# Eight byte distances between weight buffers and slots, and wider value matmuls in latent attention

## The chip, the cores and the metric

The kernel runs on one core of one Trainium2 chip. The metric is the device time of one execution in microseconds, as the median of several runs. Engines: PE (TensorE) multiplies matrices, with its weight loads shown apart as PEld; ScalarE (ACT) and VectorE (DVE) work element by element; SyncE (SP) issues the transfers.

## What is computed

One token sequence of 512 positions and 1024 features goes through two blocks in 32-bit floats. The first has two layers: a gated feed-forward, a mixer (sliding-window attention, a recurrent unit, a short convolution) and a second feed-forward. The second has one layer: a mixer of latent attention (over the 512 positions and 256 of a context) and gated linear attention, and a feed-forward with a convolution. Cut to what the change touches:

```python
def swiglu(h, w_gu, w_down):
    gu = h @ w_gu
    g, u = jnp.split(gu, 2, axis=-1)
    return (jax.nn.silu(g) * u) @ w_down
...
    def one_block(qs):
        qn, qr = qs
        s = jnp.einsum('bqhd,bkhd->bhqk', qn, k_nope) + jnp.einsum('bqhr,bkr->bhqk', qr, k_rope)
        p = jax.nn.softmax(s.astype(jnp.float32) * MLA_SCALE, axis=-1).astype(v.dtype)
        return jnp.einsum('bhqk,bkhd->bqhd', p, v)
```

Latent attention has 8 heads with values of 64 features, 512 queries in four tiles of 128, and 768 keys in six tiles of 128.

## The kernel before

**Matmuls in three parts.** Every operand of a large matmul is held as a high part (rounded to `float32r`, a copy by ScalarE, L506) and a low part (the rest, a subtraction by VectorE, L507). A product of two is three matmuls, in `mm`: low weights with high activations (L499), high with low (L500), high with high (L501), each with 128 rows, 128 output columns and up to 512 moving columns. The weights are the stationary operand, the activations the moving one.

**Weights.** They come from memory in chunks of 128 x 1024 (eight slices of 128 columns) into the four `raw` buffers, are split into one of four `whi` and one of four `wlo` buffers (pools `hip` and `lop`, `split_next`, L456 on), and are used by 24 matmuls: eight slices, three each. A chunk is split as soon as an older one is retired.

**Slots.** Activations lie in 36 tiles `r0` to `r35` of 128 x 512 (2048 bytes in each partition), which are taken and given back in a queue, in pairs of high and low part. Eight extra slots are slices of one tile `xr` in a pool `xp` that is opened last; at other times that pool holds plain floats (`xf`).

**Places in a partition.** Pools follow one another in the order in which they are opened: `cp` (the arena of 61,440 bytes, the 36 slots, and then 5,376 bytes of small tiles), `rawp`, `hip`, `lop`, `sm` (12 small tiles, 384 bytes), and `xp` behind. Tiles are rounded up to 32 bytes.

**Latent attention** (`Mixer2.mla`). For the values, `tokmajor` makes six tiles of 128 keys x 512 (L1430 to L1432 and the copy behind them). A unit is a head and a tile of 128 queries; 32 units run in the order of head pair, query tile, head. In a loop over `n`, unit `n` gets its scores (L1745, L1746: six matmuls into a pair of PSUM banks), its maximum (L1749, L1750, VectorE) and its exponentials with their sum (L1752, shown as L400, ScalarE); unit `n - 1` is divided by its sum (L1756, L1757, VectorE); unit `n - 2` is turned, by six transposes on PE (L1762) and one copy by ScalarE (L1765) into a buffer of its own. Every second step `values` (L1773) multiplies two turned units with the values of their two heads, 12 matmuls of 128 columns with 64 output columns each, which write the two halves of the partitions of one bank; the trace has two records for each. Behind the fourth query tile the bank is split into a pair of slots. In between come the keys and queries of the next head pair (`prep_k`, `prep_q`, `split_k`). `Mixer1.values` (L1167) has matmuls of the same kind with 512 columns.

Of the kernel before, what the change touches and what calls it, by code (L numbers as in the profile page):

```python
# [9 lines left out]
F32 = mybir.dt.float32  # L10
F32R = mybir.dt.float32r
AF = mybir.ActivationFunctionType
# [15 lines left out]
P = 128  # L28
S = 512
# [172 lines left out]
class Arena:  # L202


    def __init__(self):
        self.tiles = []
        self.free = []
        self.cur = 0
# [133 lines left out]
class Prog:  # L342
# [4 lines left out]
    def __init__(self, es, tc, d, out):  # L347
        self.es, self.tc, self.d, self.out = es, tc, d, out
        nc = self.nc = tc.nc
        self.T, self.V, self.A = nc.tensor, nc.vector, nc.scalar  # L350

        def mk(n, b, **k):
            return es.enter_context(tc.tile_pool(name=n, bufs=b, **k))

        cp = self.cp = mk("cp", 1)
        self.rawp = mk("rawp", self.RAW)
        self.hip = mk("hip", self.WB)
        self.lop = mk("lop", self.WB)
        self.sm = mk("sm", 12)
        self.banks = Banks(tc)  # L360
        self.park = mk("dp", 1, space=bass.MemoryType.DRAM).tile([KD, P, S], F32, name="park")
        self.logits = mk("dl", 1, space=bass.MemoryType.DRAM).tile([16, P, S], F32, name="logits")
        self.F = Arena()
        self.F.add(cp.tile([P, self.NF * 512], F32, name="farena"), self.NF * 2)
        self.R = Slots([cp.tile([P, S], F32R, name=f"r{i}")[:, :] for i in range(36)])
        self.RX = Slots()
        self.xpool = None
        self.vecs = cp.tile([P, d["vecs"].shape[1]], F32, name="vecs")
        self.cst = cp.tile([P, 3 * P], F32, name="cst")
        self.ident = self.cst[:, 0:P]  # L370
        self.maskf, self.maskb = self.cst[:, P:2 * P], self.cst[:, 2 * P:3 * P]
        self.ones = cp.tile([P, P], F32, name="ones")
        self.eps = cp.tile([P, 1], F32, name="eps")
        self.sinks = cp.tile([P, 16], F32, name="sinks")
        self.nsink = cp.tile([P, 16], F32, name="nsink")
        self.mod = [cp.tile([P, 72], F32, name=f"mod{l}") for l in range(2)]
        self.mod2 = cp.tile([P, 48], F32, name="mod2")
        self.modc = cp.tile([P, 16], F32, name="modc")
        self.crow = [None] * 3
        self.units = []  # L380
        self.ready = {}
        self.ld = self.sp = self.tk = self.rt = self.nsplit = 0
        self.bg = []
        self.users, self.loader = [], None
# [69 lines left out]
    def split_next(self):  # L454
        u = self.units[self.sp]
        if self.ld <= self.sp:  # L456
            self.load_next()
        kind, ap, key, raw = u
        n = ap.shape[-1]
        if kind == "w":  # L460
            h = self.hip.tile([P, 1024], F32R, name="whi", tag="whi")
            lo = self.lop.tile([P, 1024], F32R, name="wlo", tag="wlo")
            self.split(raw[:, :n], h[:, :n], lo[:, :n])
            self.ready[self.nsplit] = (key, h, lo)
            self.nsplit += 1
        else:
            self.mod_unit(key, raw)
            if self.sp < EARLY:
                raw.done()
        u[3] = None  # L470
        self.sp += 1
        ahead = self.RAW + (4 if self.sp < EARLY - 8 else 0)
        while self.ld < len(self.units) and self.ld < self.sp + ahead:
            self.load_next()
# [707 lines left out]
class Mixer2:  # L1182
# [236 lines left out]
    def tokmajor(self, keys, nk, toks, one=False):  # L1419

        p = self.p
        out = []

        def part(acc, w, j, xs):
            hi, lo = w
            for kk in range(nk):
                xh, xl = xs[j * nk + kk]
                s = slice(kk * 512, (kk + 1) * 512)
                a, z = j + kk == 0, j == len(keys) - 1 and kk == nk - 1
                p.T.matmul(acc[:, :], lhsT=xl, rhs=hi[:, s], start=a, stop=False)  # L1430
                p.T.matmul(acc[:, :], lhsT=xh, rhs=lo[:, s], start=False, stop=False)
                p.T.matmul(acc[:, :], lhsT=xh, rhs=hi[:, s], start=False, stop=z)  # L1432

        def copy(t, acc):
            o = p.f(512, one)
            if t % 2:
                p.V.tensor_copy(o[:, :], acc[:, :])
            else:
                p.A.activation(o[:, :], acc[:, :], AF.Copy)
            acc.done()  # L1440
            out.append(o)

        if one:
            w = p.take("x", *keys[0])
            for t, xs in enumerate(toks):
                acc = p.banks.get()
                part(acc, w, 0, xs)
                copy(t, acc)
                p.bgstep()
            p.retire()  # L1450
            return out
        accs = [p.banks.get() for _ in toks]
        for j, k in enumerate(keys):
            w = p.take("x", *k)
            for t, xs in enumerate(toks):
                part(accs[t], w, j, xs)
            p.retire()
        for t, acc in enumerate(accs):
            copy(t, acc)
        return out  # L1460
# [212 lines left out]
    def mla(self):  # L1673
        p = self.p
        V, A, T = p.V, p.A, p.T
        p.bg.append(self.g_qn())
        p.bgstep()
        toks = [[(a[:, t * P:(t + 1) * P], b[:, t * P:(t + 1) * P]) for a, b in self.kvn] for t in range(4)]
# [32 lines left out]
        ks = p.rslots(6)  # L1711
# [8 lines left out]
        def split_k(i, j):  # L1720
            r = slice(64 * j, 64 * j + 64)
            p.split(kb[i][r, :768], kh[j][r], kl[j][r])
            if j:
                kb.pop(i).done()
# [30 lines left out]
        def divide(s, m):  # L1755
            V.reciprocal(m[:, 2:3], m[:, 1:2])  # L1756
            V.tensor_scalar(s[:, :768], s[:, :768], m[:, 2:3], None, op0=MUL)  # L1757

        def turn(s):
            b = p.banks.pair()  # L1760
            for k in range(6):
                T.transpose(b[:, k * P:(k + 1) * P], s[:, k * P:(k + 1) * P], p.ident)  # L1762
            s.done()
            t = p.f(768)
            A.activation(t[:, :768], b[:, :768], AF.Copy)  # L1765
            b.done()
            return t

        def values(i, qt, p0, p1, o):
            for k in range(6):  # L1770
                for j, pt in enumerate((p0, p1)):
                    hd = 2 * i + j
                    T.matmul(o[64 * j:64 * j + 64, qt * P:(qt + 1) * P], lhsT=self.vt[k][:, hd * 64:hd * 64 + 64],  # L1773
                             rhs=pt[:, k * P:(k + 1) * P], start=k == 0, stop=k == 5)
            p0.done()
            p1.done()

        units = [(i, qt, j) for i in range(4) for qt in range(4) for j in range(2)]
        st, pt, o = {}, {}, {}
        prep_q(0)  # L1780
        p.banks.mode(2)
        split_k(0, 0)
        split_k(0, 1)
        for n in range(len(units) + 4):
            if n < len(units):
                i, qt, j = units[n]
                st[n] = scores(i, qt, j)
                if qt == 3 and i < 3:
                    split_k(i + 1, j)
                if (qt, j) == (3, 1):  # L1790
                    for jj in range(2):
                        for b in qs.pop((i, jj)):
                            b.done()
            if 1 <= n <= len(units):
                divide(*st[n - 1])
            if 2 <= n < len(units) + 2:
                pt[n - 2] = turn(st.pop(n - 2)[0])
            m = n - 3
            if 1 <= m <= len(units) and m % 2 == 1:
                i, qt, _ = units[m]  # L1800
                if qt == 0:
                    o[i] = p.banks.get()
                values(i, qt, pt.pop(m - 1), pt.pop(m), o[i])
                if qt == 3:
                    pr, = p.rpairs(1)
                    self.om.append(pr)
                    ob = o.pop(i)
                    p.split(ob[:, :], pr[0][:, :], pr[1][:, :])
                    ob.done()
            if n < len(units):  # L1810
                i, qt, j = units[n]
                if (qt, j) == (1, 1) and i < 3:
                    prep_k(i + 1)
                if (qt, j) == (2, 0) and i < 3:
                    prep_q(i + 1)
        p.banks.mode(8)
        for b in ks + self.vt + [self.tb]:
            b.done()
        p.drop(self.qn)
        p.drop(self.kvs)  # L1820
# [230 lines left out]
```

## Time and profile before

| | |
|---|---|
| median of 3 runs | 2720.52 us (2720.5 to 2720.85) |
| the profiled execution | 2719.37 us, of which its span is 2717.6 us |
| PE busy | 2686.7 us, 99% of the span, 13874 matmuls |
| VectorE, ScalarE busy | 1671.1 us (61%), 1022.1 us (38%) |
| mean granted TensorE clock | 0.995 |

Busy times of PE are unions over matmuls that overlap in the pipeline, so the duration of one matmul is longer than the step from its start to the start of the next one. A row of the timeline has the start in us from the start of the span, the duration, the engine, the line and the operation, and what it writes and reads.

### The profile page before, as it was taken

The page shows a single profiled execution, that of the slowest core. Times are in us where ns is not written, and L with a number is a line of the kernel's source. Part 1 is how long each engine was busy: PE and PEld are TensorE (multiplying, and loading weights), DVE is VectorE, ACT ScalarE, POOL GpSimd, SP SyncE. Part 2 cuts the span into 40 slices and gives each one's busy share as a digit, 9 for nine tenths or more (in the row PEclk, how much of TensorE's full clock was granted, in tenths as well). Part 3 has the DMA queues.
Part 4 walks back from the last instruction along what each step waited for, and adds up shares of the span by engine and source line. Part 5 has one row for each costly group of instructions (what it writes and reads, how often), then busy time and mean ns, then how long its engine had stood idle before and what let it go on. Part 6 is the DMA issues. An engine that isn't in the chain of part 4 may idle for free.

```text
span 2717.6 us, 34690 instructions
## 1 busy us (share of the span) xinstructions
PE 2686.7 (99%) x13874; PEld 2262.7 (83%) x13874; DVE 1671.1 (61%) x2854; ACT 1022.1 (38%) x1603; POOL 0.2 (0%) x4
## 2 busy tenths in 40 slices
PE   9999999999999999999999999999999999999998
PEld 7888897898888988888879888888888788988887
DVE  8554468664444744446866865474576675785666
ACT  3322237442222422223654232253444564432322
POOL 0000000000000000000000000000000000000000
PEclk9999999999999999999999999999999999999999
DMA  7544444344444444444423665423222203233231
GB/s 286 194 140 149 152 140 137 109 147 143 147 149 145 138 160 142 147 145 153 144 74 112 204 216 190 144 92 117 76 95 67 93 32 120 86 102 100 88 101 61
DMA packets 105890, 355.85 MB, mean 131 GB/s; under 512 B 11776, under 2 KB 14976, under 8 KB 105472
## 3 DMA queue, kind: packets, MB, share of 16 engines
q1 hardware_dynamic: 105728, 353.64, 39.4%
q8 instruction: 108, 1.77, 0.3%
q14 instruction: 54, 0.44, 0.1%
HBM read 345.21 MB, written 8.39 MB: 130 GB/s over the span
## 4 chain that ended last, share of the span: by engine, by line
PE 93%; DVE 4%; ACT 2%; issue 1%; DMA 0%; SPq 0%; DVEq 0%; ACTq 0%
PE pb L499 28%; PE pb L501 28%; PE pb L500 28%; PE pb L1773 1%; PE pd L1745 1%; PE pd L1762 1%; ACT farena L400 1%; PE pb L617 1%; PE pb L1167 1%; PE pb L1640 0%; DVE wlo L507 0%; PE pb L1114 0%; PE pb L1151 0%; PE pb L581 0%; PE pb L1430 0%
## 5 line engine op out<-in xcount | busy, mean ns | idle before, releaser
L499 PE MATMUL pb<-r,wlo 128*128 128x512 f32 (+1 forms) x3360 | 1236.6, 369 | 1.2 <-DVE wlo L507 1.1
L500 PE MATMUL pb<-r,whi 128*128 128x512 f32 (+1 forms) x3360 | 1229.2, 367 | 0.0
L501 PE MATMUL pb<-r,whi 128*128 128x512 f32 (+1 forms) x3360 | 1228.8, 366 | 0.0
L506 ACT ACTIVATE whi<-raw 128x1024 fp32r<-128x1024 f32 (+2 forms) x450 | 464.2, 1032 | 828.1 <-issue 448.5
L499 PEld LDWEIGHTS pb<-r,wlo 128*128 128x128 f32 x3360 | 632.8, 189 | 114.4 <-issue 7.6
L500 PEld LDWEIGHTS pb<-r,whi 128*128 128x128 f32 x3360 | 633.6, 189 | 103.7 <-issue 1.9
L501 PEld LDWEIGHTS pb<-r,whi 128*128 128x128 f32 x3360 | 633.4, 189 | 103.8 <-issue 0.2
L507 DVE TENSOR_TENSOR wlo<-raw,whi 128x1024 fp32r<-128x1024 f32 (+2 forms) x450 | 535.7, 1191 | 211.8 <-ACT whi L506 210.4
L511 DVE CUSTOM_DVE_ANT_0 raw<-raw,farena 128x1024 f32<-128x1024 f32 x176 | 215.2, 1223 | 194.9 <-DMA raw<-wmod 139.7
L676 DVE SCALAR_TENSOR_TENSOR farena<-pb,mod,farena 128x512 f32<-128x512 f32 (+1 forms) x176 | 114.9, 653 | 210.5 <-PE pb L501 210.2
L499 PE MATMUL pb<-xr,wlo 128*128 128x512 f32 (+1 forms) x520 | 188.1, 362 | 0.0
L501 PE MATMUL pb<-xr,whi 128*128 128x512 f32 (+1 forms) x520 | 187.4, 360 | 0.0
L500 PE MATMUL pb<-xr,whi 128*128 128x512 f32 (+1 forms) x520 | 186.5, 359 | 0.0
L400 ACT ACTIVATE farena<-pb 128x512 f32<-128x512 f32 x93 | 55.6, 598 | 331.2 <-PE pb L501 327.2
L767 DVE TENSOR_TENSOR farena<-pb,farena 128x512 f32<-128x512 f32 x110 | 75.9, 690 | 161.1 <-PE pb L501 144.1
L819 DVE SCALAR_TENSOR_TENSOR farena<-pb,vecs,farena 128x441 f32<-128x441 f32 (+2 forms) x176 | 120.7, 693 | 42.9 <-ACT farena L811 39.6
L500 PEld LDWEIGHTS pb<-xr,whi 128*128 128x128 f32 x520 | 97.8, 188 | 16.2
L501 PEld LDWEIGHTS pb<-xr,whi 128*128 128x128 f32 x520 | 97.6, 188 | 16.2
L499 PEld LDWEIGHTS pb<-xr,wlo 128*128 128x128 f32 x520 | 97.9, 188 | 15.4
L573 ACT ACTIVATE farena<-farena 128x256 f32<-128x256 f32 (+1 forms) x97 | 44.8, 467 | 84.3 <-DVE farena L676 84.3
L644 ACT ACTIVATE r<-farena,mod 128x256 fp32r<-128x256 f32 (+1 forms) x119 | 55.3, 514 | 51.2 <-DVE farena L642 50.7
L400 ACT ACTIVATE farena<-farena 128x512 f32<-128x512 f32 (+2 forms) x89 | 50.5, 604 | 58.6 <-DVE farena L819 47.7
(275 smaller groups left out, 1856.1 us busy)
## 6 DMA issues: line engine op xcount, KB each, us to landing
raw<-gu SPq DMA_DIRECT2D x213, 512.0 KB, 3.6
raw<-wmod SPq DMA_DIRECT2D x128, 512.0 KB, 3.5
raw<-dn SPq DMA_DIRECT2D x80, 448.0 KB, 3.3
raw<-wada SPq DMA_DIRECT2D x48, 512.0 KB, 3.6
raw<-dn SPq DMA_DIRECT2D x40, 512.0 KB, 3.6
raw<-w2a SPq DMA_DIRECT2D x34, 512.0 KB, 3.5
raw<-win SPq DMA_DIRECT2D x32, 512.0 KB, 3.6
raw<-wout SPq DMA_DIRECT2D x24, 512.0 KB, 3.5
```

The costliest lines, as they stand in the source:

```text
L400: i = self.A.activation(out, in_, func, **k).ins
L499: self.T.matmul(acc, lhsT=lo[:, s], rhs=xh[:, tok], start=i == 0, stop=False)
L500: self.T.matmul(acc, lhsT=h[:, s], rhs=xl[:, tok], start=False, stop=False)
L501: self.T.matmul(acc, lhsT=h[:, s], rhs=xh[:, tok], start=False, stop=i == n - 1)
L506: self.A.activation(hi, src, AF.Copy)
L507: self.V.tensor_tensor(lo, src, hi.bitcast(F32), op=SUB)
L511: self.V.tensor_tensor_reduce(out=out, in0=raw, in1=row, scale=1.0, scalar=0.0, op0=MUL, op1=ADD, accum_out=col)
L573: self.A.activation(t[:, :n], src, AF.Square, scale=scale)
L644: self.A.activation(hi[:, tok], t[:, :n], AF.Identity, bias=sh[:, k:k + 1])
L676: self.V.scalar_tensor_tensor(x, acc[:, :n], gate[:, d:d + 1], x, op0=MUL, op1=ADD)
L767: self.V.tensor_tensor(a[:, :], acc[:, :], g[:, :], op=MUL)
L819: self.V.scalar_tensor_tensor(o, g[:, r0 + i - 1:r1 + i - 1, c0 + j - 1:c1 + j - 1], self.v(f"cw{i}{j}", f), o, op0=MUL, op1=ADD)
```

## The change

The tiles of `hip` and `lop` become 16 floats wider (1040 in place of 1024), so that their buffers lie 4160 bytes apart in place of 4096; the low part is used from the eighth float on. A block of 96 floats is placed behind the small tiles, ahead of `xp`. With that, the weight buffers, the small tiles and the extra slots move; the 36 slots stay.

In latent attention the six value tiles become slices of one buffer. The turned units of a head pair go into two buffers (one for each head) of six times 512 columns, in which each unit has its 128 columns of each key tile. `values` runs once for a head pair, when its eight units are turned: 12 matmuls of 512 columns, behind the scores and the division of that step and ahead of the transposes.

```diff
+        mk("gap", 1).tile([P, 96], F32, name="gap")
...
-            h = self.hip.tile([P, 1024], F32R, name="whi", tag="whi")
-            lo = self.lop.tile([P, 1024], F32R, name="wlo", tag="wlo")
+            h = self.hip.tile([P, 1040], F32R, name="whi", tag="whi")
+            lo = self.lop.tile([P, 1040], F32R, name="wlo", tag="wlo")[:, 8:1032]
...
+            self.vbuf = p.f(512 * len(toks), True)
             for t, xs in enumerate(toks):
                 acc = p.banks.get()
                 part(acc, w, 0, xs)
-                copy(t, acc)
+                copy(t, acc, self.vbuf[:, t * 512:(t + 1) * 512])
...
-        def turn(s):
+        def turn(s, qt, j):
...
-            t = p.f(768)
-            A.activation(t[:, :768], b[:, :768], AF.Copy)
+            A.activation(pt[j][:, :].rearrange("p (k t) -> p k t", t=S)[:, :, qt * P:(qt + 1) * P],
+                         b[:, :768].rearrange("p (k t) -> p k t", t=P), AF.Copy)
             b.done()
-            return t
-
-        def values(i, qt, p0, p1, o):
+
+        def values(i):
+            o = p.banks.get()
             for k in range(6):
-                for j, pt in enumerate((p0, p1)):
+                for j in range(2):
                     hd = 2 * i + j
-                    T.matmul(o[64 * j:64 * j + 64, qt * P:(qt + 1) * P], lhsT=self.vt[k][:, hd * 64:hd * 64 + 64],
-                             rhs=pt[:, k * P:(k + 1) * P], start=k == 0, stop=k == 5)
-            p0.done()
-            p1.done()
+                    T.matmul(o[64 * j:64 * j + 64, :], lhsT=self.vt[k][:, hd * 64:hd * 64 + 64],
+                             rhs=pt[j][:, k * S:(k + 1) * S], start=k == 0, stop=k == 5)
+            pr, = p.rpairs(1)
+            self.om.append(pr)
+            p.split(o[:, :], pr[0][:, :], pr[1][:, :])
+            o.done()
...
+        pt = [p.f(6 * S) for _ in range(2)]
...
+            if n > 2 and n % 8 == 2:
+                values(n // 8 - 1)
             if 2 <= n < len(units) + 2:
-                pt[n - 2] = turn(st.pop(n - 2)[0])
-            m = n - 3
-            if 1 <= m <= len(units) and m % 2 == 1:
-                i, qt, _ = units[m]
...
+                turn(st.pop(n - 2)[0], *units[n - 2][1:])
```

## Rows read from the trace of the kernel before

**Rows 1.** The page: busy us, share and count by engine; granted clock in 40 slices.
```profile
PE 2686.7 (99%) x13874; PEld 2262.7 (83%) x13874; DVE 1671.1 (61%) x2854; ACT 1022.1 (38%) x1603; POOL 0.2 (0%) x4
...
PEclk9999999999999999999999999999999999999999
```
**Rows 2.** The page: chain that ended last, shares of the span by line.
```profile
PE pb L499 28%; PE pb L501 28%; PE pb L500 28%; PE pb L1773 1%; PE pd L1745 1%; PE pd L1762 1%; ACT farena L400 1%; PE pb L617 1%; PE pb L1167 1%; PE pb L1640 0%; DVE wlo L507 0%; PE pb L1114 0%; PE pb L1151 0%; PE pb L581 0%; PE pb L1430 0%
```
**Rows 3.** Groups of PE by shape: count, then busy us, mean ns, idle before.
```profile
L499 PE MATMUL pb<-r,wlo 128*128 128x512 f32 x2606 | 1025.5, 394 | 0.2 <-ACT r L644 0.2
...
L499 PE MATMUL pb<-r,wlo 128*128 128x256 f32 x754 | 211.1, 285 | 1.1 <-DVE wlo L507 1.1
...
L499 PE MATMUL pb<-xr,wlo 128*128 128x512 f32 x360 | 142.3, 395 | 0.0
...
L499 PE MATMUL pb<-xr,wlo 128*128 128x256 f32 x160 | 45.7, 286 | 0.0
```
**Rows 4.** Timeline of PE, slots alone: start us, duration us, line, operands.
```profile
2399.79 0.39 PE L499 MATMUL pb<-r,wlo 128*128 128x512 f32 x1
...
2410.67 0.39 PE L499 MATMUL pb<-r,wlo 128*128 128x512 f32 x1
```
**Rows 5.** Timeline of PE, a chunk half on extra slots.
```profile
2463.88 0.40 PE L499 MATMUL pb<-xr,wlo 128*128 128x512 f32 x1
2464.12 0.39 PE L500 MATMUL pb<-xr,whi 128*128 128x512 f32 x1
2464.34 0.40 PE L501 MATMUL pb<-xr,whi 128*128 128x512 f32 x1
...
2466.67 0.39 PE L499 MATMUL pb<-r,wlo 128*128 128x512 f32 x1
...
2469.41 0.40 PE L499 MATMUL pb<-xr,wlo 128*128 128x512 f32 x1
```
**Rows 6.** Timeline of PE, 256 columns on slots.
```profile
2317.76 0.28 PE L499 MATMUL pb<-r,wlo 128*128 128x256 f32 x1
...
2329.99 0.28 PE L499 MATMUL pb<-r,wlo 128*128 128x256 f32 x1
```
**Rows 7.** Timeline, 256 columns in `prep_k`.
```profile
2178.09 0.27 PE L500 MATMUL pd<-r,whi 128*128 128x256 f32 x1
2178.20 0.28 PE L501 MATMUL pd<-r,whi 128*128 128x256 f32 x1
```
**Rows 8.** Timeline of latent attention: a unit on PE, and a group of values.
```profile
2174.77 0.50 PE L1745 MATMUL pd<-xr,r 128*128 128x512 f32 x1
...
2176.50 0.48 PE L499 MATMUL pd<-r,wlo 128*128 128x512 f32 x1
...
2180.68 1.53 PE L1773 MATMUL pb<-farena 128*64 128x128 f32 x24
...
2182.14 0.19 PEld L499 LDWEIGHTS pb<-r,wlo 128*128 128x128 f32 x1 [0.17 <-issue]
```
**Rows 9.** Timeline of PE, values of the first mixer.
```profile
470.55 1.08 PE L1167 MATMUL pb<-farena 128*64 128x512 f32 x4
471.56 0.50 PE L499 MATMUL pb<-r,wlo 128*128 128x512 f32 x1
```
**Rows 10.** Groups of latent attention (2151 to 2257 us): PE and ScalarE.
```profile
L1773 PE MATMUL pb<-farena 128*64 128x128 f32 x384 | 29.4, 279 | 2.7 <-ACT farena L1765 2.6
...
L400 ACT ACTIVATE farena<-pd,small 128x768 f32<-128x768 f32 x28 | 25.2, 900 | 7.7 <-DVE small L1750 7.0 <-DVE small L1756 0.6
L1765 ACT ACTIVATE farena<-pd 128x768 f32<-128x768 f32 x30 | 24.3, 808 | 12.3 <-PE pd L1762 11.9
...
L400 ACT ACTIVATION_READ_ACCUMULATOR farena<-pd,small 128x1 f32 x28 | 5.5, 196 | 0.0
```
**Rows 11.** Timeline at the end of latent attention.
```profile
2250.03 0.81 ACT L1765 ACTIVATE farena<-pd 128x768 f32<-128x768 f32 x1
...
2252.34 0.50 PE L499 MATMUL pb<-r,wlo 128*128 128x512 f32 x1
```

More of the change, by code (lines that the diff above doesn't have):

```diff
@@ L1432, in part, with copy @@
                 p.T.matmul(acc[:, :], lhsT=xh, rhs=hi[:, s], start=False, stop=z)
-        def copy(t, acc):
-            o = p.f(512, one)
+        def copy(t, acc, o=None):
+            o = p.f(512) if o is None else o
             if t % 2:
@@ L1763, in turn @@
             s.done()
-            t = p.f(768)
-            A.activation(t[:, :768], b[:, :768], AF.Copy)
+            A.activation(pt[j][:, :].rearrange("p (k t) -> p k t", t=S)[:, :, qt * P:(qt + 1) * P],
+                         b[:, :768].rearrange("p (k t) -> p k t", t=P), AF.Copy)
             b.done()
-            return t
-        def values(i, qt, p0, p1, o):
+        def values(i):
+            o = p.banks.get()
             for k in range(6):
-                for j, pt in enumerate((p0, p1)):
+                for j in range(2):
                     hd = 2 * i + j
-                    T.matmul(o[64 * j:64 * j + 64, qt * P:(qt + 1) * P], lhsT=self.vt[k][:, hd * 64:hd * 64 + 64],
-                             rhs=pt[:, k * P:(k + 1) * P], start=k == 0, stop=k == 5)
-            p0.done()
-            p1.done()
+                    T.matmul(o[64 * j:64 * j + 64, :], lhsT=self.vt[k][:, hd * 64:hd * 64 + 64],
[4 more added lines that the diff above has]
+            o.done()
         units = [(i, qt, j) for i in range(4) for qt in range(4) for j in range(2)]
-        st, pt, o = {}, {}, {}
+        st = {}
         prep_q(0)
         p.banks.mode(2)
+        pt = [p.f(6 * S) for _ in range(2)]
         split_k(0, 0)
         split_k(0, 1)
-        for n in range(len(units) + 4):
+        for n in range(len(units) + 3):
             if n < len(units):
@@ L1795, in mla @@
                 divide(*st[n - 1])
+            if n > 2 and n % 8 == 2:
+                values(n // 8 - 1)
             if 2 <= n < len(units) + 2:
-                pt[n - 2] = turn(st.pop(n - 2)[0])
-            m = n - 3
-            if 1 <= m <= len(units) and m % 2 == 1:
-                i, qt, _ = units[m]
[L1801 to L1809, printed above, removed]
+                turn(st.pop(n - 2)[0], *units[n - 2][1:])
             if n < len(units):
@@ L1815, in mla @@
                     prep_q(i + 1)
+        for b in pt:
+            b.done()
         p.banks.mode(8)
-        for b in ks + self.vt + [self.tb]:
+        for b in ks + [self.vbuf, self.tb]:
             b.done()
```

## The prediction

> **What bounds the kernel now.** I read the page's busy shares first: PE is busy for 99% of the span at the full granted clock, every other engine for 61% or less [rows 1]. The chain that ended last says the same: 84% of the span lies in three lines of PE, L499, L500 and L501 [rows 2]. So the time is the sum of PE's steps from one matmul to the next, and nothing else matters unless it leaves PE waiting. The groups kept apart by shape then give the counts: each of the three lines has 2606 matmuls of 512 columns and 754 of 256 with a slot of `r` as moving operand, 360 and 160 with an extra slot of `xr` [rows 3]: 7818, 2262, 1080 and 480 in all.
>
> The durations in those rows overlap, so the cost of a matmul is read from the timeline, as the distance of starts. In a stretch with slots of `r` alone, 48 matmuls take 2410.67 - 2399.79 = 10.88 us, **226.7 ns** each [rows 4]. Twelve in a row on extra slots take 2466.67 - 2463.88 = 2.79 us, **232.5 ns**; the twelve on `r` behind them 2.74 us, 228.3 ns [rows 5]. Same lines, same weight buffer, same shape: only the moving operand's place differs. With 256 columns, 102 matmuls take 12.23 us, 119.9 ns [rows 6]. Twice that less 226.7 leaves 13.1 ns, an estimate of what each matmul costs above the streaming of its columns (106.8 ns for 256).
>
> **Places.** Summing the sizes in the order of the code (tiles rounded up to 32 bytes), the high buffers begin 95,488 bytes behind the first slot of `r`, which is 373 x 256. Slots lie 2048 apart, buffers 4096, slices of a buffer 512. So today every pair of slot and weight slice stands at 0 modulo 256, and the extra slots stand 128 off. After the change, high buffer n stands at 64n and low buffer n at 32 + 64n: 0, 32, 64, ... 224. The block of 96 floats brings the extra slots to the same eight distances. That the period is 256 is a guess; the trace has only these two points, 226.7 ns at 0 and 232.5 ns at 128.
>
> **The change part by part.** (1) Wider tiles, a shift by 8 floats, and the block of 96: no instruction is added, ScalarE and VectorE write as many elements. What can move is PE's pace. Six of the eight distances are not in the trace. From below, a matmul can't go under its streaming, 213.6 ns by the estimate above; the shortest single step in the rows is some 0.22 us, between the second and third matmul on the extra slots, and the one before it is 0.24 [rows 5]. From above I take that 0.24. Why not simply the mean of all? The steps on the extra slots swing between 0.22 and 0.24 although the distance is constant, so each step depends on what the one before left, and only at distance 0 do the rows settle to an even 226.7, and only some matmuls after the switch (228.3 for the first twelve). A weight load of 128 columns reads while a moving stream passes at another rate, so from any starting distance the two pass each other several times; I expect the other distances to cost about what lies between the two known ones, not a free ride. Besides, high and low parts now stand 32 apart and every chunk of 24 matmuls changes the distance, so settling is rarer. I take the middle, **230 ns**, for all slots, nearer to neither row.
> - `r`, 512 columns: today 227.3 on average (settled 226.7, and 228.3 where an extra slot came before, most chunks without one). (230.0 - 227.3) x 7818 = +21 us.
> - `xr`, 512: (230.0 - 232.5) x 1080 = -3 us.
> - 256 columns, 2742 of them: a step of 0.11 occurs beside the mean of 0.12 [rows 6, 7]; I take no change. Ends: -10 ns, -27 us; +2 ns, +5 us.
>
> The Trainium skill speaks against all of this: its page "TensorE: Matmul & The Clock Gate", section "Step-by-step: what each phase is for", says that PE has two independent read ports and that loading the next weights takes no bandwidth from the running matmul. By that rule no distance would matter; rows 5 disagree, 232.5 against 226.7 ns.
>
> (2) Latent attention's values. Today 16 groups of 24 records of 128 columns, one every two units; after, 4 groups of 24 records of 512. Columns are the same. A group today holds PE from 2180.68 to 2182.14, 1.46 us [rows 8], so 23.4 us in all. Records of that shape with 512 columns and 64 output columns already exist in L1167: four take 471.56 - 470.55 = 1.01 us [rows 9], their entry and exit included; two heads run side by side, as in the short ones. A short group without the 0.17 us of idle at its exit is 12 pairs in 1.29 us [rows 8], 0.107 a pair; four times the columns make 0.43, so a group of 24 takes some 12 x 0.43 + 0.17 = 5.3 us (6.0 by half of the 1.01), 21.3 us in all: **-2 us**. The 2.7 us that PE waits before values now [rows 10] may go or stay. Against it: without values a unit is 2174.77 to 2176.50, 1.73 us of PE [rows 8], while ScalarE needs 0.90 + 0.20 + 0.81 = 1.91 us per unit for exponential, read-out and copy [rows 10]. So between groups ScalarE leads by 0.2 us per unit, 32 x 0.2 = 6 us at most, while during a group it runs dry, as the first copy of the next head pair has to wait until the values have read the buffer that it overwrites. Queued behind that copy on ScalarE are the next exponentials, for which VectorE and PE's transposes wait. And the last group can't start until the last copy (2250.03 + 0.81): today 1.45 us of PE follow before L499 [rows 8, 11], after 5.3, so up to +4 us, less what the earlier units saved (three groups of 1.46 us). Sum of the part: -2, +1 and +1, taken as **0**, ends -5 and +8.
>
> (3) One buffer for the six value tiles: the same copies with the same elements, on ScalarE and VectorE under PE's work; zero.
>
> Sum: +21 - 3 + 0 = **+18 us**. The profiled execution took 2719.4 us (span 2717.6), 1.1 below the median of 2720.5. From it 2737; on the median **2738.5**.
>
> **Rivals.** *Faster: clear distances.* Weight loads and moving stream mostly stay out of each other's way at distances between the two known ones. For it: single steps of 0.22 exist, and 13 ns per matmul stand above streaming, so there is something to win; against it: 128, far from 0, is worse. At 224.5 ns everywhere: -2.8 x 7818 - 8 x 1080 = -31 us, the 256-column ones at 118 another -5: 2685. It decides from the point at which the mean pace falls under 227. If the whole 13 ns went, it would be 2580; I see no row that shows such a step. The Trainium skill's page "TensorE: Matmul & The Clock Gate", section "Back-to-back issue gap", gives 512 / 2.4 + 2.5 = 215.8 ns between matmuls of 512 columns; by it the time would come near 2612, an estimate, and no row here shows such a step.
>
> *Slower still: never settling.* With another distance at each chunk and 32 bytes between low and high, all matmuls go at the extra slots' pace or a little worse, 232.5 to 235: +5.2 to +7.7 ns x 7818, +41 to +60 us: 2761 to 2780. For it: the swing on the extra slots, and the slow twelve behind each switch.
>
> *Nothing: the place doesn't matter.* The extra slots are slow for another reason (where they lie, not how far from the weights), or the layout isn't as I summed it. Then the pace stays, and the values alone remain: 2716 to 2728. For it: other distances than two were never seen. Against it: the two halves of one chunk [rows 5]. This is also the outcome by the Trainium skill's rule of two independent read ports, cited above.
>
> **How the numbers follow.** Forecast (228.5 to 232 ns, 2727 to 2755) 0.37; never settling 0.18; clear distances 0.33; nothing 0.12. About 0.2%, 5.4 us, is what a measurement of this kernel can tell from no change. Of the last case some falls outside on either side, and as much of its neighbours' edges falls inside: same 0.12, slower 0.55, faster 0.33. The forecast is 2738.5; its own range is 2727 to 2755. Both signs hold much of the chance, so the range for 8 in 10 reaches from 2680 (most of the clear case) to 2772 (half of the never-settling one).
>
> **What the next profile would show.** Right: starts of matmuls on `r` some 230 ns apart and uneven, differing from chunk to chunk in a cycle of four buffers; extra slots as fast as the others; PE still 99% busy. Wrong: an even 226.7 in every chunk (nothing), or chunks at 224 and below that outnumber slower ones (clear). For the values: four blocks of about 5.3 us, with waits of ScalarE's copy behind each. The part most likely to be wrong is the pace at the six unseen distances, where one ns is 8 us.

## The result, and the profile after

The changed kernel takes **2753.22 us** (2751.41 to 2753.59) where the kernel before takes 2720.51 (2720.11 to 2720.85): a ratio of 1.0119, with a 95% interval of 1.0106 to 1.0133, +33 us. Its profiled span is 2751.6 us, 34.0 more than that of before.

The page of the changed kernel, the same rows as [rows 1] and [rows 2]:

```profile
PE 2717.8 (99%) x13586; PEld 2243.8 (82%) x13586; DVE 1669.8 (61%) x2854; ACT 1024.0 (37%) x1603; POOL 0.2 (0%) x4
...
PEclk9999999999999999999999999999999999999999
...
PE pb L502 28%; PE pb L501 28%; PE pb L500 28%; PE pb L1775 1%; PE pd L1747 1%; ACT farena L401 1%; PE pd L1764 1%; PE pb L618 1%; PE pb L1115 1%; PE pb L1168 1%; PE pb L1642 0%; DVE wlo L508 0%; PE pb L1152 0%; PE pb L1432 0%; PE pb L1431 0%
```

PE is busy for the same 99% at the same granted clock, and the chain still lies in the three lines of `mm` (now L500 to L502). PE has 288 records fewer (the values) and is busy 31 us longer. So PE doesn't wait more; its steps are longer. One line of the code over one stretch shows by how much. The stretch taken here and for all kernels below is 336 matmuls of 512 columns on slots of `r`, one behind the other, in the second feed-forward of the first layer. First the kernel before, then the changed one; the row has the operation, the count, the shortest, median and longest duration in ns, the first and the last start in us, and the shape:

```profile
L499 PE MATMUL pb<-r,wlo x112: 389/389/396, 577.0 to 652.5; 128*128 128x512 f32 x112
```
```profile
L500 PE MATMUL pb<-r,wlo x112: 388/392/398, 583.3 to 660.5; 128*128 128x512 f32 x112
```

The line is every third matmul, so 333 steps lie between the two starts: 75.5 us before, 226.7 ns a step, as in [rows 4]; 77.2 us after, **231.8 ns**. The starts of every 24th matmul in that stretch, one weight chunk apart (timeline of PE in the changed kernel):

```profile
583.27 0.39 PE L500 MATMUL pb<-r,wlo 128*128 128x512 f32 x1
...
588.83 0.39 PE L500 MATMUL pb<-r,wlo 128*128 128x512 f32 x1
...
594.42 0.39 PE L500 MATMUL pb<-r,wlo 128*128 128x512 f32 x1
...
599.98 0.39 PE L500 MATMUL pb<-r,wlo 128*128 128x512 f32 x1
...
605.56 0.39 PE L500 MATMUL pb<-r,wlo 128*128 128x512 f32 x1
...
661.24 0.39 PE L500 MATMUL pb<-xr,wlo 128*128 128x512 f32 x1
...
664.02 0.39 PE L500 MATMUL pb<-r,wlo 128*128 128x512 f32 x1
```

Four chunks take 5.56, 5.59, 5.56 and 5.58 us where each took 5.44 before (24 x 226.7 ns): all four are slow, and they differ by little. The last two rows are twelve matmuls on extra slots, 2.78 us or 231.7 ns each, against 2.79 us in [rows 5].

**Sums over the whole span.** For the tables I went through all starts of PE in order, with the byte places of the operands from the code's layout, and averaged the step from each matmul of `mm` to the next; the some hundred steps over 0.3 us, where PE waits, are left out.

| steps | count | before, ns | after, ns | change, us |
|---|---|---|---|---|
| 512 columns on `r` | 7751 | 227.27 | 232.09 | +37.4 |
| 512 columns on `xr` | 1078 | 232.72 | 232.09 | -0.7 |
| 256 columns on `r` | 2222 | 120.38 | 118.93 | -3.2 |
| 256 columns on `xr` | 480 | 119.9 | 119.2 | -0.3 |
| latent attention, first scores to the first product behind the values | | 111.9 us | 112.9 us | +1.0 |

The sum is +34.2 us; the spans differ by 34.0.

### The profile page after: what moved, and what is told of

It is laid out like the page before. It is cut to its first block, busy times and chain, and to the rows that moved or that the text cites. A ratio compares the mean times of both kernels' runs of the same rounds, so it can differ in the third digit from the quotient of the medians.

```text
span 2751.6 us, 34099 instructions
## 1 busy us (share of the span) xinstructions
PE 2717.8 (99%) x13586; PEld 2243.8 (82%) x13586; DVE 1669.8 (61%) x2854; ACT 1024.0 (37%) x1603; POOL 0.2 (0%) x4
## 4 chain that ended last, share of the span: by engine, by line
PE 93%; DVE 4%; ACT 2%; issue 1%; DMA 0%; SPq 0%; DVEq 0%; ACTq 0%
PE pb L502 28%; PE pb L501 28%; PE pb L500 28%; PE pb L1775 1%; PE pd L1747 1%; ACT farena L401 1%; PE pd L1764 1%; PE pb L618 1%; PE pb L1115 1%; PE pb L1168 1%; PE pb L1642 0%; DVE wlo L508 0%; PE pb L1152 0%; PE pb L1432 0%; PE pb L1431 0%
## 5 line engine op out<-in xcount | busy, mean ns | idle before, releaser
L502 PE MATMUL pb<-r,whi 128*128 128x512 f32 (+1 forms) x3360 | 1244.1, 371 | 0.0
L500 PE MATMUL pb<-r,wlo 128*128 128x512 f32 (+1 forms) x3360 | 1241.0, 371 | 1.3 <-DVE wlo L508 1.2
L501 PE MATMUL pb<-r,whi 128*128 128x512 f32 (+1 forms) x3360 | 1239.3, 370 | 0.0
L500 PEld LDWEIGHTS pb<-r,wlo 128*128 128x128 f32 x3360 | 631.5, 188 | 125.7 <-issue 7.3
L502 PEld LDWEIGHTS pb<-r,whi 128*128 128x128 f32 x3360 | 631.4, 188 | 110.8 <-issue 0.2
L508 DVE TENSOR_TENSOR wlo<-raw,whi 128x1024 fp32r<-128x1024 f32 (+2 forms) x450 | 536.0, 1192 | 229.6 <-ACT whi L507 228.8
L502 PE MATMUL pb<-xr,whi 128*128 128x512 f32 (+1 forms) x520 | 187.4, 360 | 0.0
L500 PE MATMUL pb<-xr,wlo 128*128 128x512 f32 (+1 forms) x520 | 187.0, 360 | 0.0
L500 PEld LDWEIGHTS pb<-xr,wlo 128*128 128x128 f32 x520 | 97.7, 188 | 16.1
L502 PEld LDWEIGHTS pb<-xr,whi 128*128 128x128 f32 x520 | 97.7, 188 | 15.4
```

What stands on the lines that cost most here:

```text
L500: self.T.matmul(acc, lhsT=lo[:, s], rhs=xh[:, tok], start=i == 0, stop=False)
L501: self.T.matmul(acc, lhsT=h[:, s], rhs=xl[:, tok], start=False, stop=False)
L502: self.T.matmul(acc, lhsT=h[:, s], rhs=xh[:, tok], start=False, stop=i == n - 1)
L508: self.V.tensor_tensor(lo, src, hi.bitcast(F32), op=SUB)
```

## Experiments

Each kernel is the kernel before with the edit shown, and has the 336 matmuls above as its row. `shift` and `gap` are blocks that nobody uses: `shift`, ahead of `rawp`, moves all that lies behind it; `gap`, ahead of `xp`, moves the extra slots alone.

**e1, the layout alone.**

```diff
+        mk("gap", 1).tile([P, 96], F32, name="gap")
...
+            h = self.hip.tile([P, 1040], F32R, name="whi", tag="whi")
+            lo = self.lop.tile([P, 1040], F32R, name="wlo", tag="wlo")[:, 8:1032]
```

> The wider weight tiles and the block ahead of the extra slots alone; latent attention as before. Theory (the pace of PE, set by the distances, is the whole loss): 2753 to 2755 us, steps of 512-column matmuls on slots 232 ns on average against 227.3 before, the same on the extra slots. Rival (part of the loss is latent attention's new values): 2735 to 2748 us, with the rest in the other run.

Measured: 2751.05 us, ratio 1.0114 (1.0099 to 1.0129). Steps of 232.11 ns on `r`, 232.09 on `xr`.

```profile
L500 PE MATMUL pb<-r,wlo x112: 388/392/398, 582.3 to 659.5; 128*128 128x512 f32 x112
```

77.2 us for 333 steps, as in the changed kernel. The layout alone makes the loss.

**e2, latent attention's values alone** (the rest of the diff).

> Latent attention's values as in the changed kernel, weight tiles and extra slots as before. Theory (the saved switches of PE are paid back at the end, where the last group stands alone): 2718 to 2723 us, no difference that can be told from none. Rival (the values cost what the layout doesn't): 2726 us or more.

Measured: 2724.03 us (2719.27 to 2725.6), ratio 1.0009 (1.0000 to 1.0019).

```profile
L499 PE MATMUL pb<-r,wlo x112: 389/389/396, 578.3 to 653.8; 128*128 128x512 f32 x112
```

75.5 us, the steps of before. What the values cost is 2.4 us by the ratio, with an interval from nothing to 5.2; in the profile latent attention takes 113.4 us, 1.5 more than before. Seven of the ten runs of e2 have a mean granted clock of 0.993 or 0.994, against 3 of the 16 runs of the kernel before beside them; how much of the 2.4 us that makes isn't shown.

**e3, extra slots at 0, slots at 128.** Is it the extra slots' place that is slow in [rows 5], or their distance from the weights?

```diff
+        mk("shift", 1).tile([P, 32], F32, name="shift")
         self.rawp = mk("rawp", self.RAW)
...
+        mk("gap", 1).tile([P, 32], F32, name="gap")
```

> Everything from the first raw buffer on moved by 128 bytes, the extra slots by another 128: the slots of r stand 128 off from all weight buffers, the extra slots 0. Buffers 4096 apart as before. Theory (the distance modulo 256 sets the pace): the paces change places, r near 232.6 ns, extra slots near 226.7 to 228 ns, time 2753 to 2760 us. Rival (the extra slots are slow by where they lie): r stays at 227.3 ns, 2720 us. Rival (only unequal distances slow PE, a constant one settles wherever it is): 2715 to 2720 us.

Measured: 2756.56 us, ratio 1.0131 (1.0111 to 1.0151). On `r` 232.93 ns, on `xr` 228.39. First the 336 matmuls, then the starts of a dozen on extra slots and of the next on `r`:

```profile
L501 PE MATMUL pb<-r,wlo x112: 390/393/404, 583.9 to 661.3; 128*128 128x512 f32 x112
```
```profile
661.99 0.40 PE L501 MATMUL pb<-xr,wlo 128*128 128x512 f32 x1
...
664.75 0.40 PE L501 MATMUL pb<-r,wlo 128*128 128x512 f32 x1
```

The slots of `r`, which haven't moved, now take 232.4 ns (77.4 us), and the extra slots are the faster ones, at 2.76 us for twelve. So it is the distance between weights and moving operand that counts, not the place of either. The rival "nothing" falls here.

**e4, both at 0.**

```diff
+        mk("gap", 1).tile([P, 32], F32, name="gap")
```

> The kernel before with a block of 128 bytes ahead of the extra slots, so that they stand at distance 0 as the slots do; nothing else. Theory (distance): the 1080 steps of 512 columns on extra slots go from 232.7 to some 227.3 ns and no chunk has to settle anew, -6 to -8 us: 2712 to 2715 us. Rival (place): 2720 us.

Measured: **2711.57 us**, ratio 0.9969 (0.9958 to 0.9981): faster than before. On `r` 227.03 ns, on `xr` 226.83.

```profile
L500 PE MATMUL pb<-r,wlo x112: 389/389/396, 576.6 to 652.2; 128*128 128x512 f32 x112
```
```profile
652.84 0.39 PE L500 MATMUL pb<-xr,wlo 128*128 128x512 f32 x1
...
655.56 0.39 PE L500 MATMUL pb<-r,wlo 128*128 128x512 f32 x1
```

Twelve on extra slots take 2.72 us in place of 2.79: 1078 x (232.72 - 226.83) = 6.3 us of the 9, and 7751 x (227.27 - 227.03) = 1.9 more on `r`, whose steps no longer have to settle behind an extra slot. In this kernel the weights stand at 256, 768, 1280 and 1792 modulo 2048 behind the slots and at 0, 512, 1024 and 1536 behind the extra slots; the mean steps at these eight lie between 226.6 and 227.4 ns, so among multiples of 256 I find no price.

Now two theories were open for 232.1 ns. Either each distance has a price of its own, and the changed kernel pays a mean of eight; or a change of distance costs, and any constant one would settle as 0 does. The next four kernels tell them apart.

**e5, constant: 64 for slots, 192 for extra slots.**

```diff
+        mk("shift", 1).tile([P, 16], F32, name="shift")
...
+        mk("gap", 1).tile([P, 48], F32, name="gap")
```

> The kernel before with two unused blocks, so that all weight buffers begin 64 bytes (modulo 256) behind all slots and 192 bytes behind all extra slots; one distance for a whole stretch, nothing else changed. Theory 'each distance has its own price', with the steps of the changed kernel (231.8 ns to a weight half at 64, 230.2 at 192): 7751 x (231.8 - 227.3) = +35 us and 1078 x (230.2 - 232.7) = -3 us, 2753 us. Theory 'it is the change of distance from one matmul to the next that costs': a constant distance settles as 0 does, 229 ns or less at both: +13 - 4 or less, 2729 us or below. The rival 'only distances 0 and 128 are special' gives the first number too, but with steps that don't depend on 64 or 192.

Measured: 2750.1 us, ratio 1.0107 (1.0077 to 1.0136). On `r` 233.21 ns, on `xr` 229.25.

```profile
L501 PE MATMUL pb<-r,wlo x112: 388/396/399, 582.1 to 659.8; 128*128 128x512 f32 x112
```
```profile
660.48 0.39 PE L501 MATMUL pb<-xr,wlo 128*128 128x512 f32 x1
...
663.23 0.39 PE L501 MATMUL pb<-r,wlo 128*128 128x512 f32 x1
```

A constant 64 doesn't settle below: 77.7 us, 233.3 ns, without a single change of distance in the stretch. The twelve on extra slots, at 192, take 2.75 us, 229.2 ns each. With 256 columns, 64 is the cheaper one: 116.5 ns on `r` against 120.4 at 0, which takes back 8.6 us.

**e6, constant: 32 and 160** (blocks of 8 and 56 floats in the same two places).

> The same with 32 bytes behind the slots and 160 bytes behind the extra slots, the two dearest distances of the changed kernel (237.2 and 236.5 ns). Theory 'each distance has its own price': 7751 x (237.2 - 227.3) = +77 us and 1078 x (236.5 - 232.7) = +4 us, 2801 us. Theory 'the change of distance costs': 229 ns or less at both, 2729 us or below. In between, about 232 ns at both, if odd multiples of 32 bytes never settle but have no price of their own: +36 us, 2757 us.

Measured: 2763.26 us, ratio 1.0155 (1.0125 to 1.0184). On `r` 233.30 ns, on `xr` 233.97.

```profile
L501 PE MATMUL pb<-r,wlo x112: 394/396/397, 584.8 to 662.5; 128*128 128x512 f32 x112
```

Again 77.7 us. Neither of the first two expectations: 32 has a price, but not the 237 ns that the changed kernel's single steps to its low halves show. A single step between two kinds of weights depends on both, so such steps are no price list; the mean over a stretch is.

**e7, the distance changes from chunk to chunk only.** High and low buffer n both at 64n.

```diff
+        mk("gap", 1).tile([P, 32], F32, name="gap")
...
+            h = self.hip.tile([P, 1040], F32R, name="whi", tag="whi")
+            lo = self.lop.tile([P, 1040], F32R, name="wlo", tag="wlo")
```

> High buffer n and low buffer n both at 64n bytes behind the slots, and the same behind the extra slots: the distance changes from one weight chunk to the next (24 matmuls) but not within a chunk. Theory 'each distance has its own price' (230.3, 231.8, 231.6, 230.2 ns in the changed kernel at 0, 64, 128, 192): a mean of 231.0: +29 us and -2 us, 2748 us. Theory 'the change of distance costs': some 9 of the 24 steps at 232 ns until it settles, the rest at 227 to 229 ns, a mean of about 229.5: +17 - 3, 2734 us.

Measured: 2742.0 us, ratio 1.0077 (1.0048 to 1.0106). On `r` 230.71 ns, on `xr` 230.56. The starts of every 24th matmul:

```profile
582.41 0.39 PE L500 MATMUL pb<-r,wlo 128*128 128x512 f32 x1
...
587.90 0.39 PE L500 MATMUL pb<-r,wlo 128*128 128x512 f32 x1
...
593.50 0.39 PE L500 MATMUL pb<-r,wlo 128*128 128x512 f32 x1
...
599.10 0.40 PE L500 MATMUL pb<-r,wlo 128*128 128x512 f32 x1
...
604.57 0.39 PE L500 MATMUL pb<-r,wlo 128*128 128x512 f32 x1
```

These four chunks stand, by the layout, at 192, 128, 64 and 0, and take 5.49, 5.60, 5.60 and 5.47 us: 228.8, 233.3, 233.3 and 227.9 ns a step. Over the whole span the chunks at 0, 64, 128 and 192 take 227.7, 233.3, 232.7 and 229.3 ns, within 0.7 of what each takes alone (227.0, 233.2, 232.9, 229.3). A change every 24 matmuls costs next to nothing; each chunk pays its own price.

**e8, the distance changes inside a chunk only.** High at 0, low at 32.

```diff
+        mk("gap", 1).tile([P, 32], F32, name="gap")
...
+            lo = self.lop.tile([P, 1088], F32R, name="wlo", tag="wlo")[:, 8:1032]
```

> All high buffers at 0 and all low buffers at 32 bytes behind the slots, and the same behind the extra slots: the distance changes only within a chunk, between the two of three matmuls that use a high half and the one that uses a low one. Theory 'each distance has its own price': (2 x 230.3 + 237.2) / 3 = 232.6 ns: +41 us, 2762 us. Theory 'the change of distance costs': as much as in the changed kernel, 232 ns, 2757 us. If it is the number of different distances that costs (eight in the changed kernel, two here), clearly less: 229 to 230 ns, 2734 to 2741 us.

Measured: 2761.41 us, ratio 1.0148 (1.0119 to 1.0178). On `r` 233.24 ns, on `xr` 233.35.

```profile
L500 PE MATMUL pb<-r,wlo x112: 389/389/395, 585.0 to 662.7; 128*128 128x512 f32 x112
```

77.7 us once more, although two of three matmuls use weights at 0. The mean of the two prices would be (2 x 227.0 + 233.3) / 3 = 229.1 ns. My numbers for the two theories were 5 us apart, too close to choose between them; beside e5 to e7 it says that 0 isn't cheap where the next matmul's weights stand elsewhere.

**e9, constant: 96 and 224**, the two that were missing (blocks of 24 and 40 floats).

> One constant distance again, 96 bytes behind all slots and 224 behind all extra slots, the two of the changed kernel's eight that no run has held alone. So far a constant distance costs 227.0 ns (0), 233.3 (32), 233.2 (64), 232.9 (128), 234.0 (160), 229.3 (192). If the changed kernel's 232.1 is the plain mean of its eight distances, two steps of three to a high half (0, 64, 128, 192: mean 230.6) and one to a low half, then 96 and 224 must cost 236.6 ns on average: about 2780 us. If they cost 230 to 234 like their neighbours (2735 to 2765 us), the plain mean is 231 or less and changing the distance inside a chunk costs the rest.

Measured: 2766.18 us, ratio 1.0166 (1.0122 to 1.0209). On `r` 234.22 ns, on `xr` 233.01.

```profile
L501 PE MATMUL pb<-r,wlo x112: 389/397/401, 585.1 to 663.1; 128*128 128x512 f32 x112
```

78.0 us, 234.2 ns. Both cost as their neighbours do and not 236.6, so the plain mean of the changed kernel's eight prices is below its 232.1; the next section works it out, for all and for each pair of buffers.

**e10, high at 0, low at 192**, the two cheapest.

```diff
+        mk("gap", 1).tile([P, 32], F32, name="gap")
...
+            h = self.hip.tile([P, 1088], F32R, name="whi", tag="whi")[:, 0:1024]
+            lo = self.lop.tile([P, 1088], F32R, name="wlo", tag="wlo")[:, 48:1072]
```

> All high buffers at 0 and all low buffers at 192, the two cheapest distances, for slots and extra slots alike. If the steps are the plain mean of the two prices, (2 x 227.0 + 229.3) / 3 = 227.8 ns on 7750 and 1078 steps: some 7 us more than with 0 alone (2711.6), 2715 to 2720 us. If changing the distance inside a chunk has a price of its own, as much as in high 0, low 32 (233.2 ns where the mean of the two prices was 229.1, 4 ns more): 231.8 ns, about 2750 us.

Measured: 2744.05 us, ratio 1.0086 (1.0063 to 1.0109). 231.11 ns on `r` and on `xr`.

```profile
L500 PE MATMUL pb<-r,wlo x112: 389/395/403, 581.1 to 658.1; 128*128 128x512 f32 x112
```

77.0 us, where the mean of the two prices, 227.8 ns, would make 75.9. Mixing them inside a chunk costs 3.3 ns a step, as 0 with 32 costs 4.1.

**e11, no multiple of 32: 16 for slots, 240 for extra slots.**

```diff
+        mk("gap", 1).tile([P, 40], F32, name="gap")
...
+            h = self.hip.tile([P, 1088], F32R, name="whi", tag="whi")[:, 4:1028]
+            lo = self.lop.tile([P, 1088], F32R, name="wlo", tag="wlo")[:, 4:1028]
```

> One constant distance that is no multiple of 32: 16 bytes behind all slots, 240 behind all extra slots. If the price follows 32-byte or 64-byte blocks, 16 costs as 0 does (227 ns) and 240 as 224: 2710 to 2720 us. If only an exact 0 is cheap, 233 ns on r: 7751 x 6 = +46 us on 2711.6, about 2757 us.

Measured: 2756.07 us, ratio 1.0129 (1.0085 to 1.0172). On `r` 232.97 ns, on `xr` 229.04.

```profile
L500 PE MATMUL pb<-r,wlo x112: 392/395/396, 583.1 to 660.8; 128*128 128x512 f32 x112
```

77.7 us: sixteen bytes off are as dear as sixty-four.

**e12, each size at its own distance.** 0 for all, but chunks that serve 256 columns alone are written 64 bytes into their buffers.

```diff
+        mk("gap", 1).tile([P, 32], F32, name="gap")
...
+            a = 16 if (65 <= self.nsplit <= 72 or 89 <= self.nsplit <= 96 or 157 <= self.nsplit <= 164
+                 or 225 <= self.nsplit <= 232 or 249 <= self.nsplit <= 256 or 317 <= self.nsplit <= 320
+                 or 378 <= self.nsplit <= 385 or self.nsplit >= 446) else 0
+            h = self.hip.tile([P, 1088], F32R, name="whi", tag="whi")[:, a:a + 1024]
+            lo = self.lop.tile([P, 1088], F32R, name="wlo", tag="wlo")[:, a:a + 1024]
```

> A version to beat both kernels: the extra slots at 0 like the slots (2711.6 us alone), and each chunk that is used only with 256-column matmuls has both of its halves written 64 bytes into its buffer. A constant 64 took 116.5 ns for a 256-column matmul where 0 takes 120.4; the distance changes only from one run of chunks to the next. If the price goes with the distance of the chunk at hand: some 1900 of 2222 steps on r and 480 on the extra slots x 3 to 4 ns = 7 to 9 us less than 2711.6, 2702 to 2705 us. If the changes between stages cost the 512-column steps anything, it shows as r above 227.0 ns; if 256 columns have no price by distance, 2711.6 us.

Measured: **2705.88 us** (2703.45 to 2706.85), ratio 0.9950 (0.9936 to 0.9963). The 336 matmuls, and the stretch of 102 with 256 columns of [rows 6]:

```profile
L503 PE MATMUL pb<-r,wlo x112: 389/389/395, 573.3 to 648.8; 128*128 128x512 f32 x112
```
```profile
2305.17 0.28 PE L503 MATMUL pb<-r,wlo 128*128 128x256 f32 x1
...
2317.18 0.28 PE L503 MATMUL pb<-r,wlo 128*128 128x256 f32 x1
```

512 columns keep the 226.7 ns of 0 (75.5 us), and the 102 take 12.01 us in place of 12.23. Over the span the 256-column steps take 117.7 on `r` and 117.9 on `xr`, some 8 us less than in e4 in all, with 227.04 for 512 columns; the medians of e4 and e12 differ by 5.7 us. It beats both kernels.

## Why the prediction was right in its sign and short in its size

The measured 2753.2 us lies inside the range of 2727 to 2755, 2 us from its upper end and 15 us above the forecast of 2738.5.

The price of a 512-column step by constant distance (the weights' place less the moving operand's, in bytes), from the runs above, as the mean over the span:

| distance, modulo 256 | 0 | 16 | 32 | 64 | 96 | 128 | 160 | 192 | 224 | 240 |
|---|---|---|---|---|---|---|---|---|---|---|
| ns | 227.0 | 233.0 | 233.3 | 233.2 | 234.2 | 232.9 | 234.0 | 229.3 | 233.0 | 229.0 |
| from | e4 r | e11 r | e6 r | e5 r | e9 r | e3 r | e6 xr | e5 xr | e9 xr | e11 xr |

Slots and extra slots agree within 0.3 ns at 0 in e4 (227.03 and 226.83) and at 128 (232.93 in e3, 232.72 before). But extra slots come in short runs between steps on `r`: in e3, where those stand at 128, the extra slots at 0 take 228.4 and not 227. So the prices that come from `xr` alone are less certain, by a ns or so; of these, 192 was seen on `r` too, in e7 (229.3).

**The pace (part 1), mis-sized.** That the distance counts, that 0 is the cheapest and that six new ones cost more was right. The size was not: +21 us on `r` was foretold, +37.4 came. The step that failed is "I take the middle, 230 ns ... nearer to neither row". Five of the six unseen distances cost 233.0 to 234.2, as 128 does or more; only 192 lies between the two known rows. Two high halves of three matmuls and one low half give (2 x (227.0 + 233.2 + 232.9 + 229.3) / 4 + (233.3 + 234.2 + 234.0 + 233.0) / 4) / 3 = 231.6 ns; the changed kernel has 232.1. So the plain mean of the prices makes 231.6 - 227.3 = 4.3 ns, some 33 us, of the loss, and 0.5 ns, 4 us, is left over.

That holds for the sum alone. By pairs of a high and a low buffer, which the starts of four chunks in the section on the result show in the order (192, 224), (128, 160), (64, 96), (0, 32), the changed kernel takes these means on `r` over the span:

| pair | (0, 32) | (64, 96) | (128, 160) | (192, 224) |
|---|---|---|---|---|
| measured, ns | 232.5 | 231.7 | 233.1 | 231.1 |
| plain mean of its prices, ns | 229.1 | 233.5 | 233.3 | 230.5 |

The cycle of four buffers that the prediction named is there, but mixing makes one pair 3.4 ns dearer than its mean and another 1.8 ns cheaper, and the differences nearly cancel. That the plain mean comes so near the total is in part luck. The prices at constant distance show that distance makes the loss; the pace of a mixed pair they do not give, and no run here shows what sets it.

**The reasons for it, half right.** "Each step depends on what the one before left" holds inside a chunk (e8, e10). That "every chunk of 24 matmuls changes the distance, so settling is rarer" matters, does not hold: in e7 that costs next to nothing. And "from any starting distance the two pass each other several times", so that the others would cost something between, was a picture without a row; a constant 16, 32, 64 or 96 is dear from end to end. Two points and an idea of what lies between them were not enough for a middle; one kernel with another constant distance would have shown 230 to be too low for most places.

**Extra slots, -3 us foretold, -0.7 came:** the same 2 ns of pace. The sign that they would be as fast as the slots came true, 232.09 ns both.

**256 columns, 0 foretold, -3.5 us came,** inside the ends of -27 and +5. e5 shows that its best distance is another than that of 512 columns.

**Values (part 2), 0 foretold.** The spans say +1.0 us for latent attention in the changed kernel and +1.5 in e2; the time of e2 lets 0 to 5. A group of the changed kernel (timeline of PE and ScalarE; the last number is the wait before it):

```profile
2195.14 1.07 PE L1775 MATMUL pb<-farena 128*64 128x512 f32 x2
...
2196.14 0.55 PE L1764 MATMUL pd<-cst,farena 128*128 128x128 f32 x3
...
2196.62 5.36 PE L1775 MATMUL pb<-farena 128*64 128x512 f32 x22
...
2201.91 0.55 PE L1764 MATMUL pd<-cst,farena 128*128 128x128 f32 x3
2202.02 0.60 ACT L507 ACTIVATE r<-pb 128x512 fp32r<-128x512 f32 x1 [4.54 <-PE pb L1775]
```

The first two records stand alone, with three transposes behind them, and take 2196.14 - 2195.14 = 1.00 us; the other 22 take 2201.91 - 2196.62 = 5.29 us. That is 6.3 us and not 5.3, some 25 us for four groups. But the 1.46 us of a short group was that of an unbroken one, and others were broken up too: summed over the steps from each record of values to the next start on PE, the values take 29.8 us before and 26.0 in the changed kernel. So the saving of 2 us came, as 3.8. PE gives it back in waits ahead of the transposes, 1.5 us before and 6.5 in the changed kernel, more than half of them for ScalarE's exponentials, as the prediction's sentence on what queues behind the copy has it. The groups of the transposes, first before, then changed (busy us, mean ns, idle us before them and what ended it):

```profile
L1762 PE MATMUL pd<-cst,farena 128*128 128x128 f32 x192 | 26.9, 275 | 1.5 <-ACT farena L400 1.3
```
```profile
L1764 PE MATMUL pd<-cst,farena 128*128 128x128 f32 x192 | 27.8, 277 | 6.5 <-ACT farena L401 3.5 <-DVE small L1752 1.6 <-DVE small L1758 0.7
```

So 0 was about right as a sum, of terms that were each too small. ScalarE runs dry as foretold, but in the split of the group's result, 4.5 us, not in the copies: their waits fall from 11.9 us [rows 10] to 8.3. And the last group stands alone at the end, as foretold:

```profile
2273.96 0.81 ACT L1766 ACTIVATE farena<-pd 128x768 f32<-128x768 f32 x1
...
2274.82 5.36 PE L1775 MATMUL pb<-farena 128*64 128x512 f32 x22 [0.74 <-ACT farena L1766]
...
2280.12 0.50 PE L500 MATMUL pb<-r,wlo 128*128 128x512 f32 x1
```

From the last copy's end (2274.77) 5.35 us follow to the next product; before it was 2252.34 - 2250.84 = 1.5 [rows 11]. These 3.85 us are the +4 of the prediction; up to the end of the last copy the changed kernel is 2.9 us ahead. Part 3, the one buffer, shows nowhere.

**The rivals.** *Never settling* had the size nearest to the result (232.5 ns at its lower end, 232.1 came) with the wrong cause: the dear pace stands at constant distances too. *Clear distances* fell for 512 columns: of ten distances none is below 0's. For 256 columns it is true at 64. (The 2580 us for "the whole 13 ns" doesn't follow from the counts: 13.1 ns x 11,640 matmuls is 152 us, which leaves 2568; no chance rests on it.) *Nothing* fell with e3. The Trainium skill's page "TensorE: Matmul & The Clock Gate", section "Step-by-step: what each phase is for", has PE read weights and moving operand through two independent ports, without one taking from the other. The same matmuls at 226.7 and 233.3 ns, with nothing changed but the bytes between their operands, speak against the rule as the prediction used it, that no distance would matter; no row shows the ports themselves. Its section "Back-to-back issue gap" gives the 215.8 ns as the gap of an isolated matmul, and some 131 ns for a sustained stream of 512-column matmuls with weight loads; neither shows in a long stretch of these kernels, whose lowest is 226.7.

**Open:** why 0, 192 and 240 are cheap, why 256 columns prefer 64, and what sets the pace of a mixed pair. What was measured is the price by distance; no row shows the reads themselves. Whether the period is 256 was tried only for multiples of 256 (e4).

## What to carry to other kernels

When PE is busy for 99% of the span, compare the starts of the same matmuls with operands in different places: 6 ns on each of 8829 steps of 512 columns is 53 us, 2% of the kernel, and shows in no busy share. Before spreading buffers over distances, measure one constant distance at a time, and once with high and low parts mixed; here aligning everything (0 modulo 256, one unused block of 128 bytes) gained 9 us, and spreading cost 33. A pace that lies between two known points should be taken from a run; here the middle was wrong for five places of six.

## What the runs showed of the hardware

- A 512-column step with another weight load in each takes 226.7 ns at its best here (336 matmuls in 75.5 us) and 233.3 in the same stretch at 16, 32 and 64, with 0 and 32 mixed as well. The granted clock in these stretches is 1.00, that is 2.4 GHz, at which these are 544 and 560 cycles; that five layouts give two values, 16 cycles apart, I had not expected.
- The steps repeat: before, other stretches of 216 or 336 matmuls of this kind, far apart in time, take 226.73 to 226.75 ns.
- The order matters within a chunk and not between chunks: 0 and 192, cheap each (227.0 and 229.3), make 231.1 when high and low halves alternate, and 0 and 32 make 233.2, but 0, 64, 128 and 192 in turn, 24 matmuls each, make their plain mean (230.7 against 230.6).
